# A two-layer encoder on one core: 4 KB of scratch for dynamic DMA descriptors instead of 16 KB, and seven raw weight buffers instead of four

## The chip, the core and the metric

The kernel runs on one core of a Trainium2 chip. TensorE (PE) multiplies matrices, its weight loads (PEld) overlap with the matmuls; VectorE (DVE) and ScalarE (ACT) do elementwise work and empty the PSUM banks into which TensorE writes; GpSimd (POOL) does small things here and issues some DMAs; SyncE (SP) issues nearly all other DMAs. Each engine works through its own queue in order, and waits by semaphores for what others must have done. All DMAs run on the core's 16 DMA engines.

The metric is the device time of one execution in microseconds (us); lower is better.

## The reference

x is 256 tokens of 2048 channels, 16 learned tokens are put in front, so there are 272 columns. There are two layers, all in float32:

```
h = rmsnorm(x)
q, k, v, f, ga, gf = split(h @ W_in)           # 6656 columns
a = attention(rope(rmsnorm(q)), rope(rmsnorm(k)), v) @ W_attn_br
s = real(fft2(f per group)) @ W_four
x = x + (sigmoid(ga + b) * a + sigmoid(gf + b) * s) @ W_out
h = rmsnorm(x)
x = x + (silu(conv3(h @ W_up_gate)) * (h @ W_up_val)) @ W_down     # 5632 hidden channels
```

The first 16 columns are dropped at the end. There are 947 chunks of 512 KB of weights, and of sums made from them, to load: the kernel is a stream of weight chunks through TensorE.

## The kernel before

**Chunks.** The weights are cut into chunks of 128 x 4 x 256 float32: 512 KB, 4 KB in each SBUF partition. The list `order` holds the groups of matmuls of the whole program and `chunks` their chunks in order of use, 947 loads. A group such as ("ug", i) goes through its chunks j, and for each of them does 24 matmuls into two PSUM banks.

**Splits.** Float32 products are made from three products of a faster type (float32r). Each chunk is split in two: ScalarE casts the raw chunk to a high half `wh` (L280), VectorE subtracts it from the raw chunk, which gives the low half `wl` (L283). A matmul group does high by high, high by low and low by high (L352 to L354). `wh` and `wl` have three buffers each. The raw buffer is free when `wl` is made.

**The pipeline.** Before the matmuls of chunk i, `next_split` calls `advance(i + 1 + LOOK)`, with LOOK = 2. That emits the loads up to chunk i + 2 + RAW on SP's queue, and puts the splits up to chunk i + 2 on a list, `todo`, from which `pump` takes one piece after each pair of matmuls. RAW is the number of raw buffers:

```
250        while st["raw"] < min(upto + RAW + 2 * (upto > first_mix), len(chunks)):
251            load_raw(st["raw"])
```

So the last load that a call emits waits for the split of chunk i + 2, the one that the same call puts on the list.

**Order.** The code states the work in program order, and the framework lays out each engine's queue from it by its own estimate of what is ready when, except where the code says `keep_in_program_order`, or `manual_schedule` for whole engines. It also allots the buffers of a pool.

**Folds.** In layer 0 the chunks of w_four (the groups "s", L368 to L394) are first folded by VectorE, two sums into a tile `wpm` with one buffer (L268 to L272), and that is split. The fold stands in the code just ahead of the chunk's split. After the matmuls of such a group ScalarE and VectorE empty its banks (L1182 to L1188). A group "s" has two chunks; between two of them come a gate group (ga or gf, four chunks) and a group "a" (two chunks, w_abr).

**The start.** The first two groups run interleaved (`first_groups`, L396). SP's queue begins with parts of x (`XT`) and chunks 0 to 3. At the first of its steps `advance(2)` emits more loads, then the last quarter of x and a mask follow (L429, L430), both kept in program order. The remaining constants come after these groups (L716 to L720).

**Sums made by DMA.** POOL issues copies and accumulations from DRAM to DRAM of 1 MB each (`weight_sums`, L533 to L557), which make sums of weights (`fv`, `ft`) for layer 1's seven-product scheme. Each is issued behind a tick, a tiny copy on POOL that reads the latest `wl`. These are the program's only DMAs from POOL, and those whose descriptors stand in the scratch that the change makes smaller.

**The mixed stretch.** In layer 1, from `first_mix` on, chunks for the products (`ps_p`, L1390) are mixed among those of the groups. There every third chunk goes to a pool of its own, `raw5`, with two buffers (L240 to L243), and two more loads are emitted ahead (L250).

Of the kernel before, what the change touches and what calls it, by code (L numbers as in the profile page):

```python
# [158 lines left out]
def encoder_kernel(ctx, tc, xT, params, consts, bmat, cfold, csign, w_fl, w_f64c, w_in, w_abr, w_four, w_f64, w_out, w_up, w_down, w_vn, w_dn, w_dt, out):  # L159
    nc = tc.nc  # L160
# [71 lines left out]
            chunks.append(ch)  # L232
    st = {"raw": 0, "fetch": 0, "next": 0, "grp": 0}
    raws, splits = {}, {}
    RAW, LOOK = 4, 2

    def load_raw(i):
        src, n = chunks[i]
# [1307 lines left out]
```

## Time and profile before

| | |
|---|---|
| runs, median (lowest to highest of 3) | 2542.17 us (2540.26 to 2542.8) |
| span of the profiled execution | 2544.3 us |
| TensorE busy | 2528.2 us, 99% |
| VectorE, ScalarE, GpSimd busy | 1825.0, 1319.8, 132.3 us |
| moved by DMA | 660.69 MB, mean 260 GB/s |
| of these from SP's queue | 538.07 MB |
| of these from POOL's queue | 117.45 MB |

The profile is of one execution. Its span goes from the first to the last instruction of the program. "Busy" is time in which an engine works at an instruction; issuing a DMA or waiting is not busy time. Rows of waits read "who waited <- whom it waited for: us in total, times, longest". Rows of timelines read "start, duration, engine, line, operation, out<-in, count", and in brackets the idle time of the engine before, with what ended it. L280 is line 280 of the kernel; a trailing q (SPq) is an engine's instruction queue. The chain of waits goes back from the last instruction of the program, at each step to what released it.

### The profile page before, as it was taken

To read this page: it belongs to the slowest core of one execution; us is meant where nothing else is said; L and a number is where in the kernel's file an instruction comes from. 1 tells how busy PE (TensorE), PEld (TensorE's weight loads), DVE (VectorE), ACT (ScalarE), POOL (GpSimd) and SP (SyncE) were. 2 spreads that over 40 slices of the span, in tenths; PEclk is the share of its full clock that TensorE was granted. 3 is DMA by queue.
4 is the path that set the end of the run, shared out by engine and by line. 5 is a ranking of instruction groups with operands and counts; after the bars stand their busy time and mean duration, and the time that the engine had idled before them with its cause. 6 is when DMAs were issued, how large, how long until landed. Compare 5 with 4: busy or idle time off the path is not lost.

```text
span 2544.3 us, 47646 instructions
## 1 busy us (share of the span) xinstructions
PE 2528.2 (99%) x18992; PEld 2447.4 (96%) x18992; DVE 1825.0 (72%) x2889; ACT 1319.8 (52%) x1893; POOL 132.3 (5%) x265
## 2 busy tenths in 40 slices
PE   9999999999999999999999999999999999999999
PEld 8999999999999999999999999999988999888987
DVE  7687766776666556666558877666778778777788
ACT  5455434554444334444445555444676566656565
POOL 0000100000000000000000000000000000000000
PEclk9999999999999999999999999999999999999999
DMA  6546889989989998999875646887889888887787
GB/s 238 163 156 217 261 270 288 280 262 302 308 271 305 300 306 274 281 318 294 252 247 183 201 150 209 246 266 240 260 293 282 298 274 285 288 286 264 240 268 261
DMA packets 171215, 660.69 MB, mean 260 GB/s; under 512 B 19424, under 2 KB 24672, under 8 KB 170096
## 3 DMA queue, kind: packets, MB, share of 16 engines
q1 hardware_dynamic: 152528, 538.07, 61.3%
q0 software_dynamic: 17024, 117.45, 18.7%
q8 instruction: 149, 2.44, 0.4%
q10 hardware_dynamic: 1440, 2.13, 0.2%
q14 instruction: 74, 0.61, 0.1%
HBM read 635.91 MB, written 136.31 MB: 304 GB/s over the span
## 4 chain that ended last, share of the span: by engine, by line
PE 86%; DMA 2%; DVE 1%; ACT 1%; issue 0%; ACTq 0%; DVEq 0%
PE ps_p L1390 10%; PE ps_ug L353 7%; PE ps_ug L354 7%; PE ps_ug L352 7%; PE ps_uv L348 4%; PE ps_d L353 3%; PE ps_uv L353 3%; PE ps_d L352 3%; PE ps_uv L354 3%; PE ps_d L354 3%; PE ps_uv L352 3%; PE ps_o L353 2%; PE ps_o L354 2%; PE ps_o L352 2%; PE ps_uv L349 2%; PE ps_gf L354 2%
## 5 line engine op out<-in xcount | busy, mean ns | idle before, releaser
L283 DVE TENSOR_TENSOR wl<-raw,wh 128x1024 fp32r<-128x1024 f32 (+1 forms) x937 | 1129.7, 1217 | 567.5 <-ACT wh L280 559.5
L280 ACT CAST wh<-raw 128x1024 fp32r<-128x1024 f32 (+1 forms) x937 | 976.0, 1046 | 890.8 <-PE ps_ug L353 201.2
L353 PE MATMUL ps_ug<-xHL,wh 128*128 128x272 f32 (+1 forms) x1408 | 401.9, 285 | 0.0
L354 PE MATMUL ps_ug<-xHL,wl 128*128 128x272 f32 (+1 forms) x1408 | 401.4, 285 | 0.4 <-DVE wl L283 0.4
L352 PE MATMUL ps_ug<-xHL,wh 128*128 128x272 f32 (+1 forms) x1408 | 400.8, 285 | 0.0
L353 PEld LDWEIGHTS ps_ug<-xHL,wh 128*128 128x128 f32 x1408 | 264.7, 188 | 3.2
L352 PEld LDWEIGHTS ps_ug<-xHL,wh 128*128 128x128 f32 x1408 | 264.6, 188 | 3.2
L354 PEld LDWEIGHTS ps_ug<-xHL,wl 128*128 128x128 f32 x1408 | 264.7, 188 | 0.6 <-DVE wl L283 0.6
L353 PE MATMUL ps_uv<-xHL,wh 128*128 128x272 f32 x704 | 203.3, 289 | 0.0
L353 PE MATMUL ps_d<-gHL,wh 128*128 128x272 f32 x704 | 202.9, 288 | 0.0
L352 PE MATMUL ps_d<-gHL,wh 128*128 128x272 f32 x704 | 202.9, 288 | 0.0
L354 PE MATMUL ps_uv<-xHL,wl 128*128 128x272 f32 x704 | 202.6, 288 | 0.0
L352 PE MATMUL ps_uv<-xHL,wh 128*128 128x272 f32 x704 | 202.3, 287 | 0.0
L354 PE MATMUL ps_d<-gHL,wl 128*128 128x272 f32 x704 | 202.1, 287 | 0.0
L1390 PE MATMUL ps_p<-wh,opnd 128*128 128x512 f32 x688 | 187.8, 394 | 0.0
L348 PE MATMUL ps_uv<-xHL,wh 128*128 128x512 f32 x448 | 159.8, 395 | 0.0
L353 PE MATMUL ps_o<-mL,wh 128*128 128x272 f32 (+1 forms) x512 | 146.6, 286 | 1.3 <-DVE mL L1205 1.3
L352 PE MATMUL ps_ga<-xHL,wh 128*128 128x272 f32 (+1 forms) x512 | 147.8, 289 | 0.0
L352 PE MATMUL ps_gf<-xHL,wh 128*128 128x272 f32 (+1 forms) x512 | 146.9, 287 | 0.1
L354 PE MATMUL ps_gf<-xHL,wl 128*128 128x272 f32 (+1 forms) x512 | 146.0, 285 | 0.4 <-DVE wl L283 0.4
L353 PE MATMUL ps_ga<-xHL,wh 128*128 128x272 f32 (+1 forms) x512 | 146.1, 285 | 0.0
L353 PE MATMUL ps_gf<-xHL,wh 128*128 128x272 f32 (+1 forms) x512 | 146.1, 285 | 0.0
(372 smaller groups left out, 5871.4 us busy)
## 6 DMA issues: line engine op xcount, KB each, us to landing
raw<-in_w_up SPq DMA_DIRECT2D x320, 512.0 KB, 5.2
raw<-in_w_in SPq DMA_DIRECT2D x191, 512.0 KB, 4.2
raw<-in_w_down SPq DMA_DIRECT2D x88, 512.0 KB, 5.4
raw<-ft SPq DMA_DIRECT2D x80, 512.0 KB, 4.8
raw<-in_w_out SPq DMA_DIRECT2D x64, 512.0 KB, 5.6
ft<-in_w_dn POOLq DMA_DIRECT2D x30, 1024.0 KB, 12.0
raw<-in_w_dn SPq DMA_DIRECT2D x60, 512.0 KB, 4.7
raw<-in_w_abr SPq DMA_DIRECT2D x32, 512.0 KB, 4.8
```

Source lines behind the costliest of these rows:

```text
L280: nc.scalar.copy(h[:, a:b], r[:, a:b])
L283: nc.vector.tensor_tensor(lo[:, a:b], r[:, a:b], h[:, a:b].bitcast(F32), op=ALU.subtract)
L348: nc.tensor.matmul(o2, h[:, c, sl], ab, start=kt == 0, stop=False)
L349: nc.tensor.matmul(o, lo[:, c, sl], ab[:, 0, :], start=False, stop=kt == nk - 1)
L352: nc.tensor.matmul(o, h[:, c, sl], a, start=kt == 0, stop=False)
L353: nc.tensor.matmul(o, h[:, c, sl], b, start=False, stop=False)
L354: nc.tensor.matmul(o, lo[:, c, sl], a, start=False, stop=kt == nk - 1)
L1390: nc.tensor.matmul(ps[h], x, w[:, 512 * h:512 * h + 512], start=fresh and (s_, q) in BEGIN and first, stop=(s_, q) in END and end, skip_gr ...
```

## The change

The scratch for dynamic DMA descriptors goes from its default, 16 KB in each SBUF partition, to 4 KB. RAW goes from 4 to 7: three more buffers of 4 KB in each partition. RAW stands in the allocation of the raw tiles (L243, L459, L464) and in the number of loads that `advance` emits ahead (L250). The first four chunks are loaded by hand as before (L459 to L470), and `raw5` keeps its two buffers.

```
@@ -232,7 +232,7 @@
     st = {"raw": 0, "fetch": 0, "next": 0, "grp": 0}
     raws, splits = {}, {}
-    RAW, LOOK = 4, 2
+    RAW, LOOK = 7, 2
...
@@ -1535,7 +1535,7 @@
-    nc = _bacc.Bacc("TRN2", target_bir_lowering=False, num_devices=1)
+    nc = _bacc.Bacc("TRN2", target_bir_lowering=False, num_devices=1, dynamic_dma_scratch_size=4096)
```

More of the change, by code (lines that the diff above doesn't have):

```diff
@@ L234, in encoder_kernel @@
     raws, splits = {}, {}
-    RAW, LOOK = 4, 2
+    RAW, LOOK = 7, 2
     def load_raw(i):
@@ L1537 @@
     }
-    nc = _bacc.Bacc("TRN2", target_bir_lowering=False, num_devices=1)
+    nc = _bacc.Bacc("TRN2", target_bir_lowering=False, num_devices=1, dynamic_dma_scratch_size=4096)
     args = [nc.dram_tensor(f"in_{n}", v.shape, mybir.dt.from_np(v.dtype), kind="ExternalInput").ap()
```

## The prediction

> **What bounds the kernel now.** I read the page first, for the share of the span in which TensorE works, then the list of who waited for whom for TensorE alone, then the chain of waits for what lies behind the longest of them.
>
> ```profile
> span 2544.3 us, 47646 instructions
> PE 2528.2 (99%) x18992; PEld 2447.4 (96%) x18992; DVE 1825.0 (72%) x2889; ACT 1319.8 (52%) x1893; POOL 132.3 (5%) x265
> ```
>
> TensorE is idle for 2544.3 - 2528.2 = 16.1 us. No number of raw buffers can win more than that, plus what an idle stretch does to its clock.
>
> ```profile
> PE ps_f L420 <- ACT wh L280: 4.7, 2, 4.4
> PE ps_a L354 <- DVE wl L283: 2.8, 2, 2.6
> PE ps_s L388 <- DVE wl L283: 1.4, 2, 0.8
> PE ps_o L353 <- DVE mL L1205: 1.3, 1, 1.3
> PE ps_fa L652 <- DVE E L631: 1.1, 1, 1.1
> PE ps_ug L354 <- DVE wl L283: 0.4, 1, 0.4
> PE ps_gf L354 <- DVE wl L283: 0.4, 1, 0.4
> PE ps_uv L349 <- DVE wl L283: 0.3, 1, 0.3
> ...
> 2540.48 0.28 PE L1467 MATMUL ps_p<-wl,tH 128*128 128x256 f32 x1
> ```
>
> These eight rows are 12.4 us, and from the end of the last matmul (2540.76) to the end of the span there are 3.5 more: together the 16.1, but for rounding. Of the 4.7 at ps_f, 4.4 is the wait for the first weights, which no buffer shortens. The others are mostly a split (wl) that comes late. The chain and the timelines say why, for the two longest:
>
> ```profile
> 265.17 9.15 DMA raw<-in_w_four
> 274.95 0.68 DVE wpm L271
> ...
> 1770.93 9.91 DMA raw<-in_w_out
> 1780.93 1.06 ACT wh L280
> ```
>
> ```profile
> 255.38 0.88 POOL L539 DMA_DIRECT2D fv<-in_w_vn  x1
> 265.71 0.50 POOL L539 DMA_DIRECT2D fv<-in_w_vn  x1 [0.25 <-issue]
> 266.94 1.22 DVE L283 TENSOR_TENSOR wl<-raw,wh 128x1024 fp32r<-128x1024 f32 x1
> 274.34 1.29 DVE L271 TENSOR_TENSOR wpm<-raw 128x512 f32<-128x512 f32 x2 [6.18 <-DMA raw<-in_w_four]
> 276.83 0.40 PE L354 MATMUL ps_a<-q,wl 128*128 128x272 f32 x1 [2.59 <-DVE wl L283]
> ```
>
> VectorE stands 6.18 us in front of a fold whose raw weights take 9.15 us to land, while POOL's 1 MB copies share the DMA engines. The code emits the split of the chunk for ps_a before that fold, but on VectorE the fold stands ahead of it; so TensorE waits 2.59 us for a split whose own data had long been there. The stall has a second part, in the granted clock:
>
> ```profile
> core 0: us, PE busy (x) PEld busy (x) DVE busy (x) ACT busy (x) POOL busy (x), PEclk, DMA share, GB/s
> 24.00:32.00 8.00, 8.00 (x67) 8.00 (x66) 6.70 (x10) 4.41 (x8) 0.00 (x0) 1.00 0.72 229
> 8.00:19.00 11.00, 10.76 (x80) 10.33 (x81) 10.14 (x22) 9.87 (x23) 0.00 (x0) 1.00 1.02 409
> 220.00:480.00 260.00, 255.40 (x2021) 253.70 (x2020) 178.69 (x287) 114.08 (x164) 23.23 (x47) 0.99 0.88 274
> 278.00:281.20 3.20, 3.20 (x16) 3.20 (x16) 1.99 (x4) 1.88 (x3) 0.06 (x1) 0.50 0.93 275
> ```
>
> Just after this wait the granted clock is 0.50 for 3.20 us: half of them, 1.6 us, is lost though TensorE counts as busy. [...]
>
> **The change part by part.** First, how much earlier a load becomes.
>
> ```profile
> L280 ACT CAST wh<-raw 128x1024 fp32r<-128x1024 f32 (+1 forms) x937 | 976.0, 1046 | 890.8 <-PE ps_ug L353 201.2
> SPq L244 <- DVE wl L283: 1177.6, 568, 6.0
> DMA to landing us min/median/max: 3.1/4.8/12.9
> ```
>
> A chunk is split every 2544.3 / 937 = 2.7 us. The SP queue waits for one thing almost always: the low half of a split, which frees a raw buffer. The load of chunk i+RAW goes out when chunk i is split, and its own split is RAW chunks later: 4 x 2.7 = 10.8 us of slack now, 7 x 2.7 = 18.9 after. The longest landing of all loads at L244 is 12.9 us. So with four buffers the slowest loads come too late, and with seven none does, if the split is where the code has it. Bytes and number of loads stay.
>
> What goes away: ps_a 2.8, ps_s 1.4 and ps_gf 0.4, each behind a fold of w_four (4.6); the half clock after the longest of them (1.6); and ps_o 1.3, where the cast at 1780.93 begins as the 9.91 us transfer lands. Sum 7.5 us. The row ps_ug (0.4) is at 1977 us, in the stretch where every third chunk has a raw5 buffer. There are still two of these, so such a chunk is loaded six chunks ahead as before; I count nothing, at best 0.4. ps_uv, ps_fa and ps_f don't hang on a late raw load and stay.
>
> Then the start. At its first call advance asks for chunks up to RAW + 2, so five loads stand in SP's queue ahead of the last quarter of x (L429) and the mask (L430), where there were two. Each waits as before for the splits of chunks 0 and 1, so the quarter is issued when it was, with three more transfers ahead of it in the engines' queues.
>
> ```profile
> 8.68 3.17 SPq L244 DMA_DIRECT2D raw<-in_w_in  x2
> 11.90 0.43 SPq L429 DMA_DIRECT2D XT<-in_xT  x1
> ...
> XT<-in_xT SPq DMA_DIRECT2D x1, 544.0 KB, 6.7
> ...
> 20.78 1.34 ACT L497 ACTIVATE xHL<-XT,prm 128x272 fp32r<-128x272 f32 x3
> 23.09 1.04 ACT L280 CAST wh<-raw 128x1024 fp32r<-128x1024 f32 x1
> 25.99 0.29 PE L422 MATMUL ps_f<-xHL,wl 128*128 128x272 f32 x1
> ```
>
> From 8 to 19 us the DMA engines are full at 409 GB/s (windows above), so three loads of 512 KB are 3 x 1.28 = 3.8 us, and x lands at 11.90 + 6.7 + 3.8 = 22.4 instead of 18.6. ScalarE wants it at 20.78 and stands 1.6 us. Queued behind that are the cast of 23.09 and its low half on VectorE (1.2 us), which would end near 27.1; TensorE reads it at 25.99. That is a stall of 1.1 us. It is 0 if the cast, whose raw chunk now lands before x, is put first, and 3.8 us if the whole delay goes through. I take 1.0: the order as it is. The backlog is gone before the constants that the fourth group needs, since from 24 to 32 us the engines are at 0.72.
>
> Last, the smaller descriptor scratch.
>
> ```profile
> q0 software_dynamic: 17024, 117.45, 18.7%
> POOL tick L538 <- DVE wl L283: 1732.2, 111, 97.0
> ```
>
> Its 112 transfers on POOL are 152 packets each in the mean, under 10 for each of 16 engines, and go out one at a time behind a tick, some 10 us apart at the closest (255.38, 265.71) with 12 us to landing: at most two are in flight. If the ring held just one, POOL would stand for two or three us, hidden in the 1732 us that it waits for ticks anyway; without that cover the sums would be late by as much, and the loads of ft with them. The trace has no price for a full ring; between zero and those us I take zero, as two transfers are far from a quarter of a ring that never showed a wait. [...]
>
> The sum: -4.6 - 1.6 - 1.3 + 1.0 = -6.5 us, a span of 2537.8. The profiled span stands 2.1 us above the median of the runs (2542.17), so the median becomes 2535.7. With the bounds: -7.9 (ps_ug too, nothing lost at the start) is 2534.3; -7.5 + 3.8 = -3.7 is 2538.5.
>
> **The rivals.**
>
> *The folds move with their loads.* A fold stands where the order on VectorE expects its raw data; with loads three chunks earlier that place may move up too, and POOL's copies make the load late there just as well.
>
> ```profile
> DVE wpm L271 <- DMA raw<-in_w_four: 20.7, 9, 6.2
> raw<-in_w_four SPq DMA_DIRECT2D x16, 512.0 KB, 6.7
> fv<-in_w_vn POOLq DMA_DIRECT2D x12, 1024.0 KB, 11.5
> ```
>
> For it: 9 of the 32 halves of folds wait for data, though the code puts them behind splits that are ready. Against it: just after a group of ps_s VectorE is full with evacuations, so there is no hole to move up into until its next idle time, near 267, by when the earlier load has landed. Then only ps_o's 1.3 goes, and the start costs 1.0: -0.3, 2541.9.
>
> *Slower: a fold ahead of the evacuations.* If the moved fold does stand ahead of the evacuations and low halves of the group before (L1183 to L1188, L283), VectorE holds back what frees PSUM banks and what the next chunk needs. The price of one is what the trace shows for the worst, 2.6 + 1.6 = 4.2 us. There are eight groups of ps_s in layer 0. Before, all of this cost 6.2; three such groups cost 12.6, so 12.6 - 6.2 - 1.3 + 1.0 = +6.1, 2548.3. It turns slower than before at the second group (8.4 against 6.2 + 0.3). For it: any change of load times shifts an order of 47646 instructions that leaves TensorE only 16.1 us idle. Against it: VectorE is at 178.69 of 260 us there, enough to catch up.
>
> *Depth doesn't help, the engines are behind.* From 220 to 480 us the DMA engines are busy 0.88 of the time. If three more buffers only move the queue, the stalls come a little later and half of them stay: -3.8 + 1.0 = -2.8, 2539.4. Against it: they move 274 GB/s there and 409 at the start.
>
> **How the numbers follow.** The forecast 0.48; the folds that move 0.18; slower 0.24; half of it 0.10. A measurement of this kernel can tell about 0.2%, 5.1 us, from no change: below 2537.1 is faster, above 2547.3 slower. Of the forecast's own range, 2534.3 to 2538.5, some five sixths of the chance is below 2537.1: 0.42 with what is over from the other cases. Slower has 0.20, since its case may also be one group smaller; the rest, 0.38, is within. The range goes down to 2533.9 and up to 2549.0, past the three groups, leaving some 0.03 below and 0.1 above.
>
> **What would show it.** Right: the rows of TensorE's waits for ps_a, ps_s, ps_gf L354 and ps_o gone or under 0.2 us, no 0.50 clock near 278 us, no wait of VectorE at L271 for w_four, L429's transfer landing some 10.5 us after its issue and about 1 us of new wait at ps_f after 25 us; POOL's issues still 0.5 to 0.95 us long. Wrong: waits at L271 that last (the folds moved), new waits of ps_gf or ps_a behind L1183 (slower), longer POOL issues or loads of ft that wait for their sums (the ring), or a stall at ps_f of more than 2 us.

## The result, and the profile after

| | before | after |
|---|---|---|
| runs, median (lowest to highest of 5) | 2542.17 us (2540.26 to 2542.92) | 2556.83 us (2553.58 to 2558.42) |
| span of the profiled execution | 2544.3 us | 2555.1 us |
| TensorE busy, idle | 2528.2, 16.1 us | 2531.0, 24.1 us |

The changed kernel is slower: the ratio is 1.0051, with a 95% interval from 1.0041 to 1.0062. The forecast was 6.5 us in the other direction. The two profiles differ by 10.8 us and the medians by 14.7. In all runs on record the device time is 1.7 to 1.9 us longer than the span, and the profiled run of after is the median itself (2556.83 us, span 2555.1). By the same difference the profiled execution of before, with its span of 2544.3, took some 2546.1 us, an estimate, 3.9 above its median: that is the whole gap between 10.8 and 14.7.

The page of the kernel after, its span and its busy times:

```profile
span 2555.1 us, 47633 instructions
PE 2531.0 (99%) x18992; PEld 2452.1 (96%) x18992; DVE 1826.1 (71%) x2889; ACT 1317.6 (52%) x1893; POOL 133.8 (5%) x265
```

Of the 10.8 us, 8.0 are more idle time of TensorE (24.1 - 16.1) and 2.8 are more busy time (2531.0 - 2528.2) for the same 18992 matmuls. The list of who waited for whom, for TensorE:

```profile
PE ps_ga L354 <- DVE wl L283: 6.2, 3, 3.2
PE ps_f L420 <- ACT wh L280: 6.0, 2, 4.4
PE ps_gf L352 <- DVE se L1183: 3.8, 1, 3.8
PE ps_ga L352 <- DVE se L1183: 3.5, 1, 3.5
PE ps_ug L354 <- DVE wl L283: 0.6, 1, 0.6
PE ps_uv L349 <- DVE wl L283: 0.3, 1, 0.3
```

The rows of ps_a (2.8), ps_s (1.4), ps_o (1.3), ps_fa (1.1) and ps_gf L354 (0.4) are gone, 7.0 us. In their place stand five stalls of the gate groups ga and gf, 6.2 + 3.8 + 3.5 = 13.5 us, two of them behind the evacuation at L1183; ps_f has 1.3 more and ps_ug 0.2. Together 15.0 - 7.0 = 8.0, which is all of the new idle time. The same list for VectorE has one row that matters, the fold of w_four that waits for its data; before it read 20.7 us in 9 waits:

```profile
DVE wpm L271 <- DMA raw<-in_w_four: 28.0, 7, 7.1
```

So the folds wait longer although the code emits their loads three chunks earlier. The chain of waits (start, duration, what) around the first new stall:

```profile
255.04 6.86 DMA raw<-in_w_four
...
261.99 0.69 DVE wpm L271
...
263.39 1.14 DVE wl L283
...
264.88 0.22 DVE se L1183
...
265.14 0.59 PE ps_gf L352
```

Read it from below: the gate group begins at 265.14, when VectorE has emptied the bank of the group ps_s before it (L1183); VectorE comes to that only after a fold, and the fold stood until 261.9 for a load issued at 255.04. Before, the load of this chunk was issued at 265.17. The timelines show the place. VectorE after:

```profile
257.70 0.43 DVE L1202 SCALAR_TENSOR_TENSOR th<-th,ps_a 128x272 f32<-128x272 f32 x1
261.99 0.69 DVE L271 TENSOR_TENSOR wpm<-raw 128x512 f32<-128x512 f32 x1 [3.86 <-DMA raw<-in_w_four]
...
263.31 1.21 DVE L283 TENSOR_TENSOR wl<-raw,wh 128x1024 fp32r<-128x1024 f32 x1
...
264.80 0.29 DVE L1183 TENSOR_TENSOR se<-ps_s,se 128x138 f32<-128x138 f32 x1
265.01 0.29 DVE L1183 TENSOR_TENSOR so<-ps_s,so 128x138 f32<-128x138 f32 x1
```

and TensorE after, at the first and the third of the five stalls:

```profile
265.14 0.59 PE L352 MATMUL ps_gf<-xHL,wh 128*128 128x272 f32 x1 [3.81 <-DVE se L1183]
...
406.06 0.39 PE L354 MATMUL ps_ga<-xHL,wl 128*128 128x272 f32 x1 [3.21 <-DVE wl L283]
```

The matmuls of ps_s end near 261.3, and their banks could be emptied at once. But VectorE stands idle for 3.86 us in front of the fold, since it works off its queue in order. ScalarE's share of the same evacuation is held with it: it waits 4.76 us for VectorE (L1203) and copies from ps_s only at 263.75. The stall costs more than its idle time, as the windows of the changed kernel show (PEclk is the granted clock):

```profile
core 0: us, PE busy (x) PEld busy (x) DVE busy (x) ACT busy (x) POOL busy (x), PEclk, DMA share, GB/s
220.00:480.00 260.00, 246.50 (x1928) 245.56 (x1927) 171.86 (x279) 110.24 (x159) 22.21 (x44) 0.97 0.82 256
265.10:270.10 5.00, 4.96 (x22) 4.96 (x23) 4.90 (x11) 1.73 (x5) 0.65 (x2) 0.50 0.75 234
293.00:297.00 4.00, 3.71 (x19) 3.71 (x20) 3.97 (x9) 1.98 (x5) 0.00 (x0) 0.64 0.72 228
406.00:410.00 4.00, 3.94 (x20) 3.94 (x21) 2.63 (x4) 0.52 (x1) 0.69 (x2) 0.59 0.85 278
```

Behind three of the five stalls the clock is halved for most of 4 or 5 us. And the first row says where the loss is: from 220 to 480 us TensorE is busy 246.50 of 260 us, where it was 255.40. It is idle 13.5 us there instead of 4.6. Outside that stretch its idle time fell, from 11.5 to 10.6 us. The start times say the same. The first matmul of ps_s (L387) begins at 235.1 us where it was 234.6, the first of layer 0's ps_uv (L352) at 565.4 where it was 553.3, and the last of ps_t (L1467) at 2550.5 where it was 2539.8. TensorE is 0.5 us behind at the first, 12.1 at the second and 10.7 at the last, so the loss is in the part of layer 0 where w_four is folded.

### The profile page after: what moved, and what is told of

Same layout as the page of the kernel before. It is cut to its first block, busy times and chain, and to the rows that moved or that the text cites. A ratio compares the mean times of both kernels' runs of the same rounds, so it can differ in the third digit from the quotient of the medians.

```text
span 2555.1 us, 47633 instructions
## 1 busy us (share of the span) xinstructions
PE 2531.0 (99%) x18992; PEld 2452.1 (96%) x18992; DVE 1826.1 (71%) x2889; ACT 1317.6 (52%) x1893; POOL 133.8 (5%) x265
## 4 chain that ended last, share of the span: by engine, by line
PE 96%; DMA 2%; DVE 1%; ACT 0%; issue 0%; SPq 0%; DVEq 0%
PE ps_p L1390 10%; PE ps_ug L353 7%; PE ps_ug L354 7%; PE ps_ug L352 7%; PE ps_uv L348 4%; PE ps_d L353 3%; PE ps_uv L353 3%; PE ps_d L352 3%; PE ps_uv L354 3%; PE ps_d L354 3%; PE ps_uv L352 3%; PE ps_o L353 2%; PE ps_o L352 2%; PE ps_o L354 2%; PE ps_gf L352 2%; PE ps_gf L353 2%
## 5 line engine op out<-in xcount | busy, mean ns | idle before, releaser
L354 PE MATMUL ps_ug<-xHL,wl 128*128 128x272 f32 (+1 forms) x1408 | 401.4, 285 | 0.6 <-DVE wl L283 0.6
L352 PE MATMUL ps_ug<-xHL,wh 128*128 128x272 f32 (+1 forms) x1408 | 400.8, 285 | 0.0
L352 PEld LDWEIGHTS ps_ug<-xHL,wh 128*128 128x128 f32 x1408 | 264.6, 188 | 3.2
L354 PEld LDWEIGHTS ps_ug<-xHL,wl 128*128 128x128 f32 x1408 | 264.7, 188 | 0.8 <-DVE wl L283 0.8
L352 PE MATMUL ps_d<-gHL,wh 128*128 128x272 f32 x704 | 202.9, 288 | 0.0
L354 PE MATMUL ps_uv<-xHL,wl 128*128 128x272 f32 x704 | 202.6, 288 | 0.0
L352 PE MATMUL ps_uv<-xHL,wh 128*128 128x272 f32 x704 | 202.3, 287 | 0.0
L354 PE MATMUL ps_d<-gHL,wl 128*128 128x272 f32 x704 | 202.1, 287 | 0.0
L354 PE MATMUL ps_ga<-xHL,wl 128*128 128x272 f32 (+1 forms) x512 | 147.7, 289 | 6.2 <-DVE wl L283 6.2
L352 PE MATMUL ps_ga<-xHL,wh 128*128 128x272 f32 (+1 forms) x512 | 149.3, 292 | 3.5 <-DVE se L1183 3.5
L352 PE MATMUL ps_gf<-xHL,wh 128*128 128x272 f32 (+1 forms) x512 | 148.0, 289 | 3.8 <-DVE se L1183 3.8
L354 PE MATMUL ps_gf<-xHL,wl 128*128 128x272 f32 (+1 forms) x512 | 146.9, 287 | 0.0
```

The source lines that it names most:

```text
L352: nc.tensor.matmul(o, h[:, c, sl], a, start=kt == 0, stop=False)
L354: nc.tensor.matmul(o, lo[:, c, sl], a, start=False, stop=kt == nk - 1)
```

## The experiments

The theory after the result: the framework puts each fold on VectorE where it expects the load to have landed. Three more buffers let the load go out earlier, so the fold moves up too, ahead of work that TensorE needs; and because POOL's 1 MB copies make the load late, VectorE stands in front of it. The rivals: the smaller scratch costs something by itself; more loads in flight crowd the DMA engines; or the single `wpm` buffer is the wait. In the three sessions the kernel before had medians of 2544.38, 2543.34 and 2543.46 us; each ratio is to the kernel before in the same session.

| kernel | ratio, 95% interval | median | profiled span |
|---|---|---|---|
| scratch 4 KB alone, four buffers | 1.0002 [0.9993, 1.0011] | 2543.54 | 2541.2 |
| seven buffers, folds kept in program order | 0.9979 [0.9970, 0.9988] | 2538.75 | 2536.4 |
| four buffers, folds kept in program order | 1.0002 [0.9993, 1.0010] | 2544.09 | 2541.1 |
| seven buffers, four loads emitted ahead until the last fold | 1.0046 [1.0031, 1.0062] | 2555.29 | 2552.7 |
| seven buffers, POOL's copies paused in the branch | 0.9983 [0.9974, 0.9992] | 2539.22 | 2538.5 |
| four buffers, the same pause | 1.0056 [1.0037, 1.0075] | 2555.76 | 2547.2 |
| six buffers, folds in order, two of `wpm` | 0.9982 [0.9973, 0.9991] | 2537.99 | 2537.1 |
| three more buffers for chunks after the last fold only | 0.9998 [0.9989, 1.0007] | 2542.03 | 2539.5 |
| five buffers, nothing else | 0.9967 [0.9955, 0.9979] | 2536.80 | 2533.8 |
| six buffers, nothing else | 1.0008 [0.9998, 1.0017] | 2546.10 | 2544.0 |
| six buffers, two of `wpm`, folds in order and one chunk earlier | 0.9961 [0.9949, 0.9974] | 2535.21 | 2534.2 |

All but the four-buffer kernels with the pause and with the folds in order have the 4 KB scratch.

**The scratch alone.**

```
-    nc = _bacc.Bacc("TRN2", target_bir_lowering=False, num_devices=1)
+    nc = _bacc.Bacc("TRN2", target_bir_lowering=False, num_devices=1, dynamic_dma_scratch_size=4096)
```

> Only the scratch of 4 KB, four raw buffers as before. Theory (the folds of w_four moved ahead on VectorE): the order of every queue is that of before, so 2542, within 2.5 us, and POOL's issues stay at 0.5 to 0.95 us. Rival (the small ring holds POOL's copies up and the sums or loads come late): slower than before, up to the 2557 of the change.

Ratio 1.0002, and nearly the pattern of the waits of before: the fold waits 18.1 us in 9, ps_a 2.2 and ps_s 1.0. The scratch costs nothing that can be measured; the loss is the buffers'.

**The folds held in their place.** RAW = 7 and the small scratch as in the change, and

```
-            nc.vector.tensor_tensor(r[:, o:o + 2], raws[i][:, 0:2], raws[i][:, 2:4], op=op)
+            tc.keep_in_program_order(nc.vector.tensor_tensor(r[:, o:o + 2], raws[i][:, 0:2], raws[i][:, 2:4], op=op))
```

> The change as it is, but the two halves of each fold keep their place in program order on VectorE. Theory: VectorE no longer waits for w_four at L271 (28.0 us after the change), the five stalls of TensorE between 258 and 480 us with their half clock (some 19 us) go, and what is left is the gain at ps_o and the cost of the start: 2536, between 2534 and 2540. Rival (three more loads in flight crowd the DMA engines, whatever the order): loads still land late and the time stays above 2550.

TensorE's waits in that kernel:

```profile
PE ps_f L420 <- ACT wh L280: 4.5, 1, 4.5
PE ps_s L388 <- DVE wl L283: 2.5, 5, 0.6
PE ps_uv L349 <- DVE wl L283: 0.3, 1, 0.3
```

The five stalls are gone, and no fold waits for its data any more. The kernel that was 0.51% slower is 0.21% faster with two instructions held in order. The same edit with four buffers:

> The kernel before with its folds kept in program order, scratch and four buffers as before. Theory: the fold's place is what costs, with four buffers too, so the waits for ps_a, ps_s and ps_gf L354 (4.6 us) and the half clock (1.6) go: 2536, with ps_o's 1.3 still there. Rival (with four buffers the load is late wherever the fold stands): 2542, the same waits.

```profile
PE ps_s L388 <- DVE wl L283: 2.8, 6, 0.6
PE ps_ug L354 <- DVE wl L283: 1.4, 2, 0.8
...
DVE wpm L271 <- DMA raw<-in_w_four: 0.7, 1, 0.7
```

This was a miss: it is not faster than before. The folds' waits go here too, but held late in the queue they make the split of their own chunk late, and ps_s waits for that (2.8 us). Against four buffers with the same folds, seven are worth 1.0002 - 0.9979 = 0.23%, and by the medians 5.3 us.

**Is that wait the single `wpm` buffer?** Six buffers, folds in order, and

```
-        r = wp.tile([P, CW, MG * P], F32, tag="wpm", name=f"wpm{i}", bufs=1)
+        r = wp.tile([P, CW, MG * P], F32, tag="wpm", name=f"wpm{i}", bufs=2)
```

> Folds kept in program order, six raw buffers, and the seventh given to a second buffer for the folded chunk. Theory (with the folds pinned, what is left in layer 0 is TensorE's 2.5 us at ps_s, since a second fold waits until the first is split): these 2.5 us go and the slack of six buffers, 16 us, is still enough: 2536 to 2538, 1 to 3 below the pinned kernel with seven. Rival (pinned folds are late by their place, not by the buffer): no difference from the pinned kernel, 2539.

```profile
PE ps_s L388 <- DVE wl L283: 2.0, 5, 0.5
```

No: ps_s still waits five times with the second buffer there, so the single buffer is not what it waits for. To the same kernel one more edit was made, which puts the fold on the list `todo` one chunk earlier:

```
-            if i in folded:
-                todo.append((i, lambda i=i: fold_w(i)))
+            for k in (i, i + 1):
+                if k in folded and k not in begun:
+                    begun.add(k)
+                    todo.append((i, lambda k=k: fold_w(k)))
```

> The pinned kernel with six raw buffers and two for folds, in which the code emits each fold one chunk earlier, still in program order. Theory (what is left at ps_s, 2.0 us, is the fold's place just ahead of its own split): these go and the time is 2536, 1 to 3 below 2538. Rival (the fold a chunk earlier meets a load that has not landed): waits at L271 come back, 2539 or more.

```profile
PE ps_f L422 <- ACT wh L282: 5.4, 3, 4.5
PE ps_uv L351 <- DVE wl L285: 0.3, 1, 0.3
```

The waits of ps_s are gone, so they came from the place of the fold; only the start and 0.3 us are left. It has the lowest median of all, at a ratio of 0.9961, though its interval overlaps that of five buffers.

**The load made punctual instead.** The change as it is, with POOL's copies stopped in layer 0's branch and made up for after it:

```
-                        slow[2] = 26 if last else 15
+                        slow[2] = 26 if last else 0
...
-                slow[2] = 22 if last else 20 if half else 15
+                slow[2] = 22 if last else 10
...
+                slow[2] = 14
```

> The change as it is, but POOL's copies and accumulations are paused through layer 0's branch groups and made up for in the output groups and layer 0's feed-forward stage. It asks whether the early place of a fold is enough, or whether its load has to be late as well. Theory (early place and a load that POOL's copies make late): w_four lands in 3.5 to 6 us, VectorE's waits at L271 fall from 28.0 to under 8 us, the waits behind L1183 go, and the time is 2538 to 2544. Rival (the early place alone costs, since two folds take 2.6 us of VectorE ahead of the evacuations): waits behind L1183 stay, 2550 or more.

Its view of the DMA issues (median us from issue to landing at the end; the kernel after has 6.5 there), then its list of waits:

```profile
raw<-in_w_four SPq DMA_DIRECT2D x16, 512.0 KB, 4.2
```

```profile
DVE wpm L271 <- DMA raw<-in_w_four: 11.9, 7, 5.6
...
PE ps_gf L352 <- DVE se L1183: 1.7, 1, 1.7
...
PE ps_ga L352 <- DVE se L1183: 0.3, 1, 0.3
```

The folds stand at the moved place, two of the stalls behind L1183 are still there, but the five that cost 13.5 us now cost 2.0. The folds' own waits fell from 28.0 to 11.9 us, not to the 8 expected. The late load is therefore the second ingredient. Either of the two, place or lateness, undone alone turns the loss into a gain. The same pause with four buffers:

> The same pause in the kernel before, with four buffers. Theory: its own waits behind folds (18 to 21 us on VectorE, 3.9 to 4.6 on TensorE) go too: 2538 to 2542, near the kernel with seven. If the copies do harm at their new place, both kernels show it alike.

```profile
PE ps_uv L354 <- DVE wl L283: 2.5, 4, 0.8
PE ps_nb L580 <- DVE dg L577: 2.1, 1, 2.1
PE ps_uv L352 <- ACT wh L280: 2.0, 1, 2.0
```

Another miss, 0.56% slower. The stalls of the branch are gone, but now groups wait between 790 and 1350 us, where the copies that are made up for run. The profile is of this kernel's fastest run (2549.04 us), 6.7 below its median, so it leaves a part of the loss unshown. With seven buffers and the copies in the same places, TensorE's list has of these only ps_nb at 0.2 and ps_o at 1.1. So with the same pause the deeper buffers take away most of these waits, as the forecast had it for plain loads.

**Fewer loads ahead, with the buffers there.** Seven buffers, but emitting only four ahead up to the last fold:

```
-        while st["raw"] < min(upto + RAW + 2 * (upto > first_mix), len(chunks)):
+        ahead = RAW if upto > max(folded) else 4
+        while st["raw"] < min(upto + ahead + 2 * (upto > first_mix), len(chunks)):
```

> Seven buffers and the small scratch, but loads run only four chunks ahead until the last fold of layer 0 has been split, then seven. Theory: start and folds as before, ps_o's 1.3 us gained: 2541, within 3. Rival (seven buffers cost elsewhere too, in layer 1 or by the scratch): 2547 or more.

```profile
PE ps_gf L353 <- DVE se L1184: 3.9, 1, 3.9
PE ps_ga L353 <- DVE se L1184: 3.6, 1, 3.6
```

A miss that taught something: the place in the code where a load is emitted does not hold it back. The folds begin as early as in the changed kernel, the first at 206.7 us (207.7 there, 220.7 before), and wait 25.1 us for their loads in 7 times (28.0 in 7 there). In the changed kernel the load of the first moved fold goes out at 255.04, within 0.03 us of the end of the fold before it (255.01), which frees a raw buffer. So what it waited for is a buffer, and the seven are there in both. The next kernel takes the buffers themselves away: the three extra ones get a tag of their own and serve only chunks behind the last fold.

```
-            r = wp.tile([P, CW, MG * P], F32, tag="raw", name=f"raw{i}", bufs=RAW)
+            x = i > max(folded) and i % 7 > 3
+            r = wp.tile([P, CW, MG * P], F32, tag="rawx" if x else "raw", name=f"raw{i}", bufs=RAW - 4 if x else 4)
```

> Small scratch and three more raw buffers, but these have a tag of their own that is used only for chunks behind the last fold of layer 0; until then four buffers in every respect. VectorE's order is that of before up to the last fold. Theory (all the loss is between 230 and 490 us): nothing is lost, ps_o's 1.3 us is gained: 2541, faster than before by 0 to 3. Rival (some of the loss is elsewhere, by the scratch's place, the start or layer 1): 2547 or more.

Ratio 0.9998, and the waits of the branch are those of before, the longest of ps_a 1.7 us. So it takes the extra buffers in the stretch of the folds to bring the five stalls. The same run says that behind that stretch three more buffers gain nothing that can be told from no change.

**Between four and seven.**

> The change with five raw buffers, nothing pinned. In VectorE's queue its folds stand behind both halves of the evacuations (L1183) of the group before. Theory: no wait of TensorE behind L1183; folds still stand ahead of splits that are ready, as before: 2540 to 2545, the same as before. Rival (each further buffer costs a share of the 13 us): 2546 to 2548.

> The change with six raw buffers, nothing pinned. The first fold stands between the two halves of the evacuations, so only the second half is held back. Theory: between five and seven, 2544 to 2552, with VectorE's waits at L271 over 10 us and TensorE's behind L1183 of 0 to 4 us in all. Rival (each further buffer costs a share): 2551 or more.

VectorE with five buffers, at the same place in the program:

```profile
260.21 0.29 DVE L1183 TENSOR_TENSOR se<-ps_s,se 128x138 f32<-128x138 f32 x1
...
263.70 0.29 DVE L1183 TENSOR_TENSOR se<-ps_s,se 128x138 f32<-128x138 f32 x1
...
267.56 0.69 DVE L271 TENSOR_TENSOR wpm<-raw 128x512 f32<-128x512 f32 x1 [1.90 <-DMA raw<-in_w_four]
```

With six:

```profile
263.67 0.29 DVE L1183 TENSOR_TENSOR se<-ps_s,se 128x138 f32<-128x138 f32 x1
...
268.60 0.69 DVE L271 TENSOR_TENSOR wpm<-raw 128x512 f32<-128x512 f32 x1 [2.49 <-DMA raw<-in_w_four]
269.21 0.29 DVE L1183 TENSOR_TENSOR se<-ps_s,se 128x138 f32<-128x138 f32 x1
```

With five the fold stands behind the evacuations of both banks, with six between them, with seven ahead of both (the timeline of after above). The folds wait in all three, 20.6 us in sum with five and 28.1 with six, but with five TensorE waits for only 0.3 us at the gate groups. That kernel is faster, 0.9967, where 2540 to 2545 us had been expected; with six the stalls, behind splits and not behind L1183, are about as large as what the buffers win:

```profile
PE ps_gf L354 <- DVE wl L283: 5.6, 3, 3.2
...
PE ps_ga L354 <- DVE wl L283: 2.4, 1, 2.4
```

## Why the prediction was wrong

**The step that failed** is the argument against "the folds move with their loads": "just after a group of ps_s VectorE is full with evacuations, so there is no hole to move up into until its next idle time, near 267". It took VectorE's measured times as the measure of where a fold can stand. The place is fixed when the queue is laid out, before anything runs, and there the earlier load was allowed to bring the fold ahead of the evacuations. VectorE then made the hole itself, by standing idle from 258.1 to 262.0. Its free time on the average was no protection: it was busy 171.86 of 260 us in the stretch, less than before, and still held TensorE up. That the framework goes by an estimated landing is inferred from how the place moves with the number of buffers and from what holding it in order does; the estimate itself is in no trace. The prediction had both halves of this, that the fold's place depends on its load and that POOL's copies make the load late; it gave the two cases built on them 0.42 together, and the forecast took the folds as staying.

**What came in its place** is the rival "a fold ahead of the evacuations". Its mechanism is the one shown, and its price of 2.6 us of stall and 1.6 of clock for a group was near: three stalls had 3.2 to 3.8 us, somewhat more. The clock took more than 1.6 behind the worst, 5.0 us at 0.50, which is 2.5 lost. The count was too small: five groups and not three. The case gave 2548.3; in place of its 12.6 us for three groups stand 13.5 of stalls and, by the three windows, 5.00 x 0.50 + 4.00 x 0.36 + 4.00 x 0.41 = 5.6 of clock, 19.1. (The busy time of the page gives 2.8 + 1.6 = 4.4 for the clock, since the 1.6 of before are gone, so 5.6 is rather too much.) The start times above give much the same: TensorE falls 12.1 - 0.5 = 11.6 us behind in the stretch, 13.5 - 4.6 = 8.9 of them idle, which leaves 2.7 and, with the 1.6 of before, 4.3 for the clock. With 19.1 the sum of that rival would be 2548.3 + 6.5 = 2554.8, and 2556.83 was measured. That is 12.6 above the kernel before, between the 10.8 of the profiles and the 14.7 of the medians.

**Depth itself: right.** The stalls at ps_a, ps_s and ps_o, which the forecast had removed, are gone, and outside the stretch of the folds no split is late by more than the 0.6 and 0.3 us of ps_ug and ps_uv. Where the folds do no harm the buffers bring about what had been forecast, 6.5 us and at best 7.9: by the medians of one session five buffers are 2543.46 - 2536.80 = 6.7 us faster than before, and seven with the folds held in order 2544.38 - 2538.75 = 5.6. Six with the folds early have 8.3, but that kernel has more edits. The rival "depth doesn't help" falls with that.

**The start: the transfer right, the stall elsewhere.** The forecast had x's last quarter land some 10.5 us after its issue instead of 6.7, and 1.0 us of wait at ps_f after 25 us. The rows of L429, of the line's own view and of TensorE's timeline:

```profile
DMA to landing us min/median/max: 10.4/10.4/10.4
```

```profile
9.18 0.40 PE L420 MATMUL ps_f<-xHL,wh 128*128 128x272 f32 x1 [1.60 <-ACT wh L280]
```

The landing is 10.4, but no wait follows it: ScalarE casts two chunks first (at 21.64 and 24.66) and takes up the quarter at 25.61, the case that the prediction had priced at 0. The 1.6 us stand at 9.18, where the last piece of chunk 0 landed 5.4 us after its issue, against 4.2 before. That does not go with the number of loads ahead. The pinned kernel with seven buffers has the same loads in the queue and no such wait (its one wait at ps_f is the 4.5 us for the first weights), and the kernel with the scratch alone has four buffers and a wait of 1.0 us (5.4 in two, the longer 4.4). The landing was 4.2 us with five buffers, and with POOL's copies paused 4.4 with four and 4.8 with seven. It is scatter of the start, as far as these runs show. A half clock came with it, which nothing in the sum had: 0.50 from 10.8 to 14.2 us, 1.7 us lost. But ps_fa's 1.1 went, and at 235 us TensorE was only 0.5 us behind.

**The scratch: right.** It costs nothing that can be measured by itself, at a ratio of 1.0002, and POOL's issues keep their 0.50 to 0.98 us. The prediction took zero for it because two transfers are far from a quarter of the ring of descriptors. That was the author's estimate: how many transfers the ring holds, and what it would cost if it were too small, no run shows.

**The profile that the sum was read from.** It showed an execution of some 2546.1 us, 3.9 above the median. The prediction set the span of 2544.3 beside the median as if both were the same measure and saw 2.1. The difference that it forecast does not change by that, but a term may: the 1.6 us for the clock near 278 us is not in every execution. 1.6 of 2544 us make a mean granted clock of 0.999, which the profile of before has. The kernel with the scratch alone waits 2.2 us at ps_a, and its mean clock is 1.0; so it is in 22 of the 27 runs of the kernel before in the first of the later sessions.

**Left open:** what made that one execution of before slower. In the later sessions the same kernel ran between 2539.63 and 2550.37 us.

## What to carry to other kernels

A deeper buffer can move the consumer as well as the load when something lays out the queues by expected landings: before adding one, look for instructions that read a transfer on an engine that also frees PSUM banks, and hold those in order. The wait of such an instruction costs nothing in itself (20.6 us with five buffers, and the kernel was faster); what is queued behind it sets the price. Try the sizes between as well: five buffers gave 0.9967, six 1.0008 and seven 1.0051.

## What the runs showed of the hardware

**The clock after a gap.** Behind TensorE's gap of 3.81 us the granted clock was 0.50 for 5 us, and behind one of 2.59 us (before, at 277 us) for 3.20. Behind 2.26 us it stayed full, as the timeline and the windows of the kernel after show:

```profile
479.33 0.39 PE L354 MATMUL ps_ga<-xHL,wl 128*128 128x272 f32 x1 [2.26 <-DVE wl L283]
```

```profile
479.30:483.30 4.00, 3.97 (x31) 3.97 (x32) 3.04 (x4) 1.36 (x2) 1.88 (x2) 1.00 0.90 297
```

But the length of the gap alone does not settle it. In the same kernel the gap of 1.60 us at the start (at 9.18) was followed by a half clock too:

```profile
10.80:14.20 3.40, 3.40 (x18) 3.40 (x17) 3.40 (x8) 3.23 (x9) 0.00 (x0) 0.50 1.02 419
```

With seven buffers and four loads ahead, where TensorE waits 3.9, 3.6, 2.5 and 2.4 us for VectorE, the mean granted clock was 0.997; with the scratch alone, where it waits 2.2 us, it was 1.0. So no bound on the gap comes out of these runs.

**A copy from DRAM to DRAM beside loads.** The 512 KB loads of w_four took 6.5 us in the median with POOL's 1 MB copies in the stretch (6.7 before, 5.2 with five buffers, 5.9 with six and two of `wpm`, 5.0 with the three more for chunks after the last fold) and 4.2 without (4.3 with four buffers). From 220 to 480 us the DMA engines of the kernel after were busy 0.82 of the time. In the four fortieths of its span from 256 to 511 us they moved 233, 278, 256 and 280 GB/s, and with the copies paused (254 to 508 us) 179, 272, 210 and 203. What slows the loads is not shown.
